# The last eight rows of a prefix-sum kernel's input loaded by SyncE's queue instead of GpSimd's

## The chip, the cores and the metric

The kernel runs on one core of one Trainium2 chip. The metric is the device time of one execution in microseconds (us). Before the change it is 668.23 us, the median of 3 runs (667.75 to 668.69). A profile of one execution comes with a trace of it.

## The reference

```python
def setup_inputs():
    B, H, W = 4, 4224, 4224
    return {"x": np.random.randn(B, H, W).astype(np.float32)}

def reference(x):
    B, H, W = x.shape
    ps = np.cumsum(np.cumsum(x, axis=1), axis=2)
    N = min(H, W)
    diag = np.diagonal(ps, axis1=1, axis2=2)
    return np.cumsum(diag, axis=1).astype(np.float32)
```

For each of four 4224x4224 matrices the two-dimensional prefix sum is taken, its diagonal is read, and the diagonal is summed up once more. Output i of a batch is therefore a sum over the diagonal entries up to i, and each of those is a sum over a square corner of the matrix. All of x (285 MB in fp32) has to be read once; the output is 4x4224 numbers.

## The kernel before

**Main part.** P is 128 and N is 4224. Rows are taken in groups of 384 (GW), of which there are 11 (NG). A strip is 768 rows, 6 on each partition, cast from fp32 to bf16 by the load itself: `load_rows` (L75) issues it on GpSimd's (POOL's) queue. The pool `strips` has three buffers (NBUF), so a load is issued when the strip three places earlier has been used up. For each strip, `add_up` lets TensorE sum columns right of the diagonal into the tile `d`, lets VectorE (DVE) mask the block on the diagonal (L353, L354), and lets ScalarE (ACT, `act_sum`, L262) and DVE (`row_sums`, L267) sum the rows left of it. After each batch a short chain over `d` gives the carries between groups and the batch's sums (L477, L479).

**The last batch** (b = 3) has four whole strips, called s = 0 to 3 here. A fifth strip buffer takes two half strips of 384 rows (h = 0 and 1). A sixth, which is the buffer of s = 2 again, takes the rest of the rows in small pieces, all on POOL's queue:

- `part_a`, two blocks of 128 rows in strip rows 0 and 1, in two loads of 2160 and 1536 columns (L433), for all but the last 528 columns, which SyncE (SP) loaded as fp32 at the very start (`head`, L68);
- `part_b`, the last 128 rows, 4096 columns (TB) of them, in strip row 2. They are four blocks of 32 rows (R). A row is cut into four pieces of 1024 columns, so that a block of 32 rows covers 128 partitions. The blocks 0, 1 and 2 are one load each. Block 3 is two loads of 768 and 256 columns (bcut), all at L444.

Strip row 3 is scratch (`spare`); rows 4 and 5 are unused.

The order of the instructions on each engine is the order in which the program writes them. On DVE the second half strip (h = 1) follows right on the `row_sums` of the first (h = 0). At the very end block 3 is summed by `act_sum` and two `pair_sum` (L276) into the three columns of `esum`; three small products with `weights4` add these to `fin_e`, the last 32 outputs; DVE copies them (L562), and SP sends them out (L563). SP's queue holds in this order: `head`, the sums of the first three batches (L540), those of the last (L543), and the three last pieces of the output (L546, L557, L563).

Of the kernel before, what the change touches and what calls it, by code (L numbers as in the profile page):

```python
# [8 lines left out]
FP32 = mybir.dt.float32  # L9
# [8 lines left out]
def kernel(  # L18
# [14 lines left out]
    nc = tc.nc  # L33

    B, H, W = x.shape
    N = H
    P = 128
# [7 lines left out]
    TB = N - P  # L45
# [7 lines left out]
    last = ctx.enter_context(tc.tile_pool(name="last", bufs=1))  # L53
# [16 lines left out]
    def strip_tile():  # L70
        return strips.tile([P, F2, N], BF16, name="strip")

    def load_rows(o, b, r0):
        f = o.shape[1]
        nc.gpsimd.dma_start(  # L75
            out=o, in_=x[b, r0 : r0 + f * P, :].rearrange("(p f) w -> p f w", f=f)
        )
# [20 lines left out]
    def upper_mask(f):  # L98
# [22 lines left out]
        out=um1,  # L121
        in_=um1,
# [10 lines left out]
        out=ident,  # L133
        in_=ident,
# [13 lines left out]
    def counted(name, rows, width, pieces):  # L148

        ti = consts.tile([P, GW], I32, name="counted")[:rows, :width]  # L150
        for c0, c1, base, step, cm in pieces:
            nc.gpsimd.iota(
                ti[:, c0:c1],
                pattern=[[step, c1 - c0]],
                base=base,
                channel_multiplier=cm,
            )
        tf = consts.tile([rows, width], FP32, name=name)
        nc.gpsimd.tensor_copy(out=tf, in_=ti)
        return tf  # L160
# [6 lines left out]
    def between_groups(name, turned):  # L167
# [25 lines left out]
    weights = counted("weights", P, GW, [(0, GW, 1, 1, -1)])  # L193
    nc.gpsimd.affine_select(
        out=weights,
        in_=weights,
# [8 lines left out]
    R = P // 4  # L205
# [3 lines left out]
        out=steps, in_=steps, scalar=2, op=ALU.arith_shift_right  # L209
    )  # L210
    weights4 = consts.tile([P, P], FP32, name="weights4")
# [5 lines left out]
    def matmul(o, lhsT, rhs, start=False):  # L217
        nc.tensor.matmul(  # L218
            o, lhsT=lhsT, rhs=rhs, start=start, stop=False, skip_group_check=True
        )  # L220
# [36 lines left out]
    def act_sum(acc, src, own=None):  # L257
        w = src.shape[-1]
        dump = own
        if dump is None:  # L260
            dump = src
        nc.scalar.activation(  # L262
            out=dump[:, :w], in_=src, func=ACT.Copy, accum_out=acc
        )

    def row_sums(acc, src):
        nc.vector.reduce_sum(out=acc, in_=src, axis=AX.X)  # L267

    pairs = []

    def pair_sum(acc, src):

        w = src.shape[-1] // 2
        pair = last.tile([P, w], FP32, name=f"pair{len(pairs)}")
        pairs.append(pair)
        nc.vector.scalar_tensor_tensor(  # L276
            out=pair[:, :w],
            in0=src[:, :w],
            scalar=1.0,
            in1=src[:, w:],  # L280
            op0=ALU.mult,
            op1=ALU.add,
            accum_out=acc,
        )
# [17 lines left out]
        nc.vector.memset(rows3[i], 0.0)  # L302


    asum = last.tile([P, 2, 2], FP32, name="asum")
    dtot = last.tile([P, 1], FP32, name="dtot")
    hu = last.tile([P, 3], FP32, name="hu")
    hmu = last.tile([P, 3, GW], BF16, name="hmu")
    for h in range(2):
        w = GW - h * P  # L310
# [6 lines left out]
    for b in range(B):  # L317
# [10 lines left out]
        def row_of(j):  # L328
            return (j + t0) % NG
# [12 lines left out]
        def add_up(strip, f, r0, acc, um, fs=0, wp=0, ws=0, by_rows=False):  # L342


            nw = f * P // GW
            g = r0 // GW
            hi = r0 + f * P
            for j in range(g + nw + by_rows, NG):
                for q in range(f):
                    columns(j, 0, GW, strip[:, q, j * GW : (j + 1) * GW], q > 0)  # L350
            mu = mup.tile([P, f, f * P], BF16, name=f"mu{f}")
            block = strip[:, :, r0:hi]
            nc.vector.tensor_mul(out=mu, in0=block, in1=um)  # L353
            nc.vector.tensor_sub(out=block, in0=block, in1=mu)  # L354
            if by_rows:
                rowed = mup.tile([P, GW], FP32, name="rowed")
                row_sums(
                    rowed,
                    strip[:, :, hi : hi + GW].rearrange("p q c -> p c q"),
                )  # L360
            for h in range(nw):
                for q in range(f):
                    columns(g + h, 0, GW, mu[:, q, h * GW : (h + 1) * GW], q > 0)
            if by_rows:
                k = row_of(g + nw)
                matmul(d, sel_f[:, NG - 1 - k : 2 * NG - 1 - k], rowed)
            if fs:
                for q in range(fs):
                    act_sum(acc[:, q : q + 1], strip[:, q, :hi])
                row_sums(acc[:, fs:], strip[:, fs:, :hi])  # L370
            else:
                for q in range(f):
                    act_sum(acc[:, q, 0:1], strip[:, q, wp:ws])
                row_sums(acc[:, :, 1], strip[:, :, ws:hi])
# [4 lines left out]
        for s in range(ns):  # L379
            strip = prefetched.pop(0) if prefetched else None  # L380
            if strip is None:
                strip = strip_tile()
# [14 lines left out]
        for h in range(2):  # L397
            ps = slice(h * HP, (h + 1) * HP)
            k = row_of(h)
            nc.vector.tensor_copy(  # L400
                out=r6[ps, k : k + 2 * ns : 2, :], in_=a6[ps]
            )

        strip = strip_tile()
        if whole:
            load_rows(strip[:, :F], b, T0)
            add_up(strip[:, :F], F, T0, r3[:, LG], um3, F - 1)
        else:


            for h in range(2):
                load_rows(strip[:, h * F : h * F + F], b, T0 - (2 - h) * GW)
            add_up(strip[:, :F], F, T0 - 2 * GW, r3[:, row_of(LG - 2)], um3, F - 1)
            ready = psum_s.tile([P, 512], FP32, name="fold")
            for i in range(28):
                matmul(ready, ident_h, um6[:, i % F2, :512], start=True)
            fold_g = psum_s.tile([P, F, 160], FP32, name="fold")
            wp, ws = 1920, 1920 + 1248
            fold_in(fold_g, strip[:, F:], 0, wp, 160, start=True)
            parts = last.tile([P, F, 3], FP32, name="parts")  # L420
            add_up(strip[:, F:], F, T0 - GW, parts, um3, wp=wp, ws=ws)
            row_sums(parts[:, :, 2], fold_g)
            row_sums(r3[:, row_of(LG - 1), :], parts)

        if not whole:

            strip = strip_tile()
            part_a = strip[:, 0:2]
            part_b = strip[:, 2, :TB].rearrange("p (s c) -> p s c", s=4)
            spare = strip[:, 3, :]  # L430
            acuts = [(1536, N - HC), (0, 1536)]
            for c0, c1 in acuts:
                nc.gpsimd.dma_start(out=part_a[:, :, c0:c1], in_=src_a[:, :, c0:c1])  # L433
            CB = TB // 4
            bcut = 768
            for sb, c0, c1 in (
                (0, 0, CB),
                (1, 0, CB),
                (2, 0, CB),
                (3, 0, bcut),  # L440
                (3, bcut, CB),
            ):
                r0 = TB + sb * R
                nc.gpsimd.dma_start(  # L444
                    out=part_b[:, sb, c0:c1],
                    in_=x[b, r0 : r0 + R, :TB].rearrange("r (k c) -> r k c", k=4)[
                        :, :, c0:c1
                    ],
                )

            fold_a = psum_s.tile([P, 2, 256], FP32, name="fold_a")
            c0, c1 = acuts[0]
            fcuts = [c0, c0 + 768, c0 + 2048, c1]
# [13 lines left out]
        c1 = mup.tile([NG, GW], FP32, name="c1")  # L467
# [10 lines left out]
        for i, (to, src) in enumerate(((c1, d), (c2, c1))):  # L478
            nc.vector.tensor_tensor_scan(  # L479
                out=to,  # L480
# [14 lines left out]
        fin_e = psum_s.tile([1, R], FP32, name="fin_e")  # L495
# [7 lines left out]
        def weigh_b(rows, w, r0=0, start=False):  # L503

            m = P - R - r0
            matmul(fin_b[:, r0:], rows, w[..., :m], start=start)
            matmul(fin_e, rows, w[..., m : m + R], start=start)


        c0, c1 = acuts[1]  # L510
# [5 lines left out]
        nc.scalar.copy(out=by, in_=by_ps)  # L516
        weigh_b(dtot, weights, start=True)
        weigh_b(ones_col[0:1], last_sums[0:1, M0:])


        row_sums(asum[:, :, 1], fold_a)
# [10 lines left out]
        esum = last.tile([P, 3], FP32, name="esum")  # L532
        act_sum(bsum[:, 0, 0:1], part_b[:, 1, :512], spare[:, :512])
        pair_sum(bsum[:, 0, 1:2], part_b[:, 1, 512:])
        for i in (1, 0):
# [5 lines left out]
            out=out[:LB, :].rearrange("b (g i) -> g b i", i=GW), in_=whole_sums  # L541
        )
        nc.sync.dma_start(  # L543
            out=out[b, :T0].rearrange("(g i) -> g i", i=GW), in_=last_sums[1:NG]
        )
        nc.sync.dma_start(  # L546
            out=out[b, T0 : T0 + M0].unsqueeze(0), in_=yl[:, :M0]
        )
        for i in (1, 0):
            weigh_b(bsum[:, 1, i : i + 1], weights4, 2 * R)  # L550


        act_sum(esum[:, 0:1], part_b[:, 3, :320], spare[:, 960:1280])
        pair_sum(esum[:, 1:2], part_b[:, 3, 320:bcut])
        pair_sum(esum[:, 2:3], part_b[:, 3, bcut:])
        nc.scalar.copy(out=yl[:, M0:E0], in_=fin_b)
        nc.sync.dma_start(  # L557
            out=out[b, T0 + M0 : T0 + E0].unsqueeze(0), in_=yl[:, M0:E0]
        )
        for k in (1, 0, 2):  # L560
            matmul(fin_e, esum[:, k : k + 1], weights4[:, :R])
        nc.vector.tensor_copy(out=ye, in_=fin_e)  # L562
        nc.sync.dma_start(out=out[b, T0 + E0 : N].unsqueeze(0), in_=ye)  # L563

# [29 lines left out]
```

## Time and profile before

| | us |
|---|---|
| median of 3 runs | 668.23 |
| the profiled execution | 667.48 |
| its span, first to last instruction | 665.4 |
| DVE busy | 334.5 (50%) |
| PE busy | 211.2 (32%) |
| ACT busy | 154.5 (23%) |
| POOL busy | 31.7 (5%) |
| traffic of POOL's load queue (q0) | 99.9% of 16 DMA engines' span |

The table is read from the bottom: no compute engine is busy for more than half of the time, while the 16 DMA engines work nearly all of it. The mean rate is 215 GB/s as written, and the HBM is read at 429 GB/s, twice as much, because the loads cast four-byte numbers to two-byte ones. The trace also holds a record of every DMA packet with its queue, size, start and duration, but not the number of the DMA engine that carried it.

### The profile page before, as it was taken

Reading aid. Unit: us, or ns where it says so; the run is one execution under the profiler, and the core shown is the slowest. Engines: PE = TensorE matmul, PEld = TensorE weight load, DVE = VectorE, ACT = ScalarE, POOL = GpSimd, SP = SyncE. Lnnn points to the kernel's source line nnn. Section 1 sums busy time; section 2 is a strip of 40 time slices with the busy share of each in tenths; the row PEclk is TensorE's granted clock in tenths of the full one; section 3 lists DMA queues with packets and bytes.
Section 4 is the critical chain, followed back from the end, with each engine's and each line's share of the span. In section 5 each row is a group of like instructions: output and inputs, shape, how many; then the busy total and the mean of one; then the engine's idle time right before and its main releaser. Section 6 shows DMA issues by size and latency. Waiting matters only on the chain.

```text
span 665.4 us, 2519 instructions
## 1 busy us (share of the span) xinstructions
PE 211.2 (32%) x997; PEld 97.2 (15%) x998; DVE 334.5 (50%) x160; ACT 154.5 (23%) x145; POOL 31.7 (5%) x60
## 2 busy tenths in 40 slices
PE   0071422303107143230311623404022253250458
PEld 0030210101103021010110311201001121120224
DVE  4141727466914163655782325456487323251746
ACT  0010203133511020322450102123154010221443
POOL 4200000000000000000000000000000000001000
PEclk9995857655558585665555957567565595765789
DMA  9999999999999999999999999999999999999998
GB/s 203 219 219 219 219 219 218 213 213 210 220 219 218 219 219 219 218 215 213 212 220 218 219 216 219 219 218 217 212 216 216 218 218 219 218 218 216 216 205 164
DMA packets 7666, 143.24 MB, mean 215 GB/s; under 512 B 698, under 2 KB 998, under 8 KB 2150
## 3 DMA queue, kind: packets, MB, share of 16 engines
q0 software_dynamic: 7312, 142.47, 99.9%
q1 hardware_dynamic: 342, 0.61, 0.3%
q8 instruction: 8, 0.13, 0.1%
q14 instruction: 4, 0.03, 0.0%
HBM read 285.47 MB, written 0.07 MB: 429 GB/s over the span
## 4 chain that ended last, share of the span: by engine, by line
DVE 42%; another core or an unknown queue 40%; DMA 11%; ACT 3%; issue 1%; PE 1%; POOL 1%; DVEq 0%; ACTq 0%; POOLq 0%
DVE acc L267 19%; DMA strip<-in_x_dram 11%; DVE mu L353 7%; DVE strip L354 7%; DVE rowed L267 7%; ACT strip L262 3%; PE d L218 0%; DVE c L479 0%; DVE whole_sums L479 0%; POOL strip L444 0%; DVE pu L267 0%; DVE whole_sums L287 0%; POOL strip L433 0%; DVE rows L400 0%
## 5 line engine op out<-in xcount | busy, mean ns | idle before, releaser
L262 ACT ACTIVATE strip<-strip 128x768 bf16<-128x768 bf16 (+9 forms) x71 | 150.3, 2118 | 481.7 <-DVE strip L354 450.8
L353 DVE TENSOR_TENSOR mu<-strip,um 128x4608 bf16<-128x4608 bf16 (+1 forms) x24 | 52.4, 2183 | 294.3 <-DMA strip<-in_x_dram 294.2
L225 PEld LDWEIGHTS <-sel 128*11 128x11 bf16 x643 | 66.5, 103 | 475.0 <-issue 445.1
L267 DVE TENSOR_REDUCE acc<-strip 128x3 f32<-128x2304 bf16 (+4 forms) x19 | 134.8, 7094 | 0.2
L218 PE MATMUL d<-strip,sel 128*11 128x384 bf16 x90 | 37.2, 413 | 286.9 <-DMA strip<-in_x_dram 286.9
L225 PE MATMUL d<-strip,sel 128*11 128x384 bf16 x441 | 115.6, 405 | 13.8 <-DMA strip<-in_x_dram 13.8
L354 DVE TENSOR_TENSOR strip<-strip,mu 128x4608 bf16<-128x4608 bf16 (+1 forms) x24 | 52.4, 2183 | 1.5
L267 DVE TENSOR_REDUCE rowed<-strip 128x384 f32<-128x2304 bf16 x12 | 49.3, 4110 | 0.0
L218 PE MATMUL d<-mu,sel 128*11 128x384 bf16 x43 | 15.9, 370 | 103.1 <-DVE mu L353 103.1
L225 PE MATMUL d<-mu,sel 128*11 128x384 bf16 x200 | 45.9, 364 | 0.0
L75 POOL DMA_DIRECT2D strip<-in_x_dram x23 | 15.7, 684 | 534.7 <-DVE acc L267 287.9
L218 PE MATMUL d<-rowed,sel_f 128*11 128x384 f32 x24 | 11.5, 568 | 21.9 <-DVE rowed L267 21.9
L267 DVE TENSOR_REDUCE rows<-strip 128x1 f32<-128x4224 bf16 (+1 forms) x4 | 17.4, 4353 | 0.1
L218 PEld LDWEIGHTS <-sel 128*11 128x11 bf16 x134 | 13.5, 101 | 22.7 <-issue 10.2
L262 ACT ACTIVATION_READ_ACCUMULATOR strip<-strip 128x1 f32 x71 | 13.2, 186 | 0.0
L218 PE MATMUL d<-ident,rows 128*11 128x128 f32 x24 | 5.7, 374 | 16.5 <-ACT strip L262 16.5
L267 DVE TENSOR_REDUCE pu<-d 11x1 f32<-11x384 f32 x4 | 2.2, 545 | 14.1 <-PE d L218 14.1
L218 PE MATMUL fold<-um,ident_h 128*128 128x512 bf16 x27 | 6.3, 392 | 0.3 <-issue 0.3
L262 ACT ACT_TABLE_LOAD x1 | 1.3, 1283 | 19.7 <-DMA strip<-in_x_dram 19.7
L102 POOL TENSOR_SCALAR_AFFINE_SELECT um<-um 128x4608 bf16<-128x4608 bf16 (+1 forms) x2 | 5.2, 2612 | 7.3 <-DVE um L101 7.3
L101 DVE MEMSET um<- 128x4608 bf16 (+1 forms) x2 | 4.9, 2458 | 1.1 <-issue 1.1
L218 PEld LDWEIGHTS d<-rowed,sel_f 128*11 128x11 f32 x24 | 1.5, 91 | 26.8 <-DVE rowed L267 26.4
(114 smaller groups left out, 75.8 us busy)
## 6 DMA issues: line engine op xcount, KB each, us to landing
strip<-in_x_dram POOLq DMA_DIRECT2D x18, 6336.0 KB, 73.5
strip<-in_x_dram POOLq DMA_DIRECT2D x7, 3168.0 KB, 57.5
strip<-in_x_dram POOLq DMA_DIRECT2D x1, 1080.0 KB, 51.6
strip<-in_x_dram POOLq DMA_DIRECT2D x1, 768.0 KB, 54.6
strip<-in_x_dram POOLq DMA_DIRECT2D x3, 256.0 KB, 55.9
head<-in_x_dram SPq DMA_DIRECT2D x1, 528.0 KB, 3.9
strip<-in_x_dram POOLq DMA_DIRECT2D x1, 192.0 KB, 43.2
strip<-in_x_dram POOLq DMA_DIRECT2D x1, 64.0 KB, 28.6
```

The source lines that it names most:

```text
L75: nc.gpsimd.dma_start(out=o, in_=x[b, r0 : r0 + f * P, :].rearrange("(p f) w -> p f w", f=f))
L101: nc.vector.memset(um, 1.0)
L102: nc.gpsimd.affine_select(out=um, in_=um, compare_op=ALU.is_gt, fill=0.0, base=0, pattern=[[-1, f], [1, f * P]], channel_multiplier=-f,)
L218: nc.tensor.matmul(o, lhsT=lhsT, rhs=rhs, start=start, stop=False, skip_group_check=True)
L225: te.add_instruction(mybir.InstMatmult(start_tensor_calc=False, stop_tensor_calc=False, tile_position=(0, 0), tile_size=(P, P if lhsT.shap ...
L262: nc.scalar.activation(out=dump[:, :w], in_=src, func=ACT.Copy, accum_out=acc)
L267: nc.vector.reduce_sum(out=acc, in_=src, axis=AX.X)
L353: nc.vector.tensor_mul(out=mu, in0=block, in1=um)
L354: nc.vector.tensor_sub(out=block, in0=block, in1=mu)
```

## The change

Of the last 32 rows of the last batch only 24 stay in block 3 on POOL's queue. The loads of that block cover 96 partitions instead of 128, and so do the sums over it. The other 8 rows (E) come by SP's queue, uncast, each row whole: 4096 fp32 numbers on one of the partitions 0 to 7, in strip rows 4 and 5 of the same sixth buffer. That buffer is now taken from the pool ahead of the first half strip's `add_up`, not behind the second's. One DVE reduction sums the 8 rows (`end_sums`), and one small product adds them to the last 8 columns of `fin_e`.

SP's load waits for what the buffer waits for, the last use of s = 2. It stands second in SP's queue, ahead of the output of the first three batches. On DVE the new reduction stands between the reduction of h = 0 and the mask of h = 1. On TensorE the new product stands ahead of the `by` products. The other engines keep their order.

```diff
-        pair = last.tile([P, w], FP32, name=f"pair{len(pairs)}")
+        pair = last.tile([P, w], FP32, name=f"pair{len(pairs)}")[: src.shape[0]]
...
+    E = 8
+    end_sums = last.tile([E, 1], FP32, name="end_sums")
...
+            tail = strip_tile()
+            ends = tail[:E, 4:6, :].rearrange("p q c -> p (q c)").bitcast(FP32)
+            nc.sync.dma_start(out=ends[:, :TB], in_=x[b, N - E : N, :TB])
             add_up(strip[:, :F], F, T0 - 2 * GW, r3[:, row_of(LG - 2)], um3, F - 1)
+            row_sums(end_sums, ends[:, :TB])
...
-            strip = strip_tile()
+            strip = tail
...
-            for sb, c0, c1 in (
-                (0, 0, CB),
-                (1, 0, CB),
-                (2, 0, CB),
-                (3, 0, bcut),
-                (3, bcut, CB),
+            for sb, rows, c0, c1 in (
+                (0, R, 0, CB),
+                (1, R, 0, CB),
+                (2, R, 0, CB),
+                (3, R - E, 0, bcut),
+                (3, R - E, bcut, CB),
             ):
                 r0 = TB + sb * R
                 nc.gpsimd.dma_start(
-                    out=part_b[:, sb, c0:c1],
-                    in_=x[b, r0 : r0 + R, :TB].rearrange("r (k c) -> r k c", k=4)[
-                        :, :, c0:c1
-                    ],
+                    out=part_b[: 4 * rows, sb, c0:c1],
+                    in_=x[b, r0 : r0 + rows, :TB].rearrange(
+                        "r (k c) -> r k c", k=4
+                    )[:, :, c0:c1],
                 )
...
+        matmul(fin_e[:, R - E :], end_sums, weights[:E, :E])
...
-        act_sum(esum[:, 0:1], part_b[:, 3, :320], spare[:, 960:1280])
-        pair_sum(esum[:, 1:2], part_b[:, 3, 320:bcut])
-        pair_sum(esum[:, 2:3], part_b[:, 3, bcut:])
+        PE = 4 * (R - E)
+        act_sum(esum[:PE, 0:1], part_b[:PE, 3, :320], spare[:PE, 960:1280])
+        pair_sum(esum[:PE, 1:2], part_b[:PE, 3, 320:bcut])
+        pair_sum(esum[:PE, 2:3], part_b[:PE, 3, bcut:])
...
         for k in (1, 0, 2):
-            matmul(fin_e, esum[:, k : k + 1], weights4[:, :R])
+            matmul(fin_e, esum[:PE, k : k + 1], weights4[:PE, :R])
```

## The prediction

> **What bounds the kernel now.** I read the page from the back: the DMA queues first, because the DMA row of the slices is full, then the chain, then the last microseconds in the timeline.
>
> ```profile
> DMA  9999999999999999999999999999999999999998
> q0 software_dynamic: 7312, 142.47, 99.9%
> q1 hardware_dynamic: 342, 0.61, 0.3%
> q8 instruction: 8, 0.13, 0.1%
> ```
>
> POOL's queue (q0) fills all 16 DMA engines for the whole span. SP's queue (q1) and the instruction fetches (q8) share the same engines. So the bound is the work of the DMA engines, and bytes moved from q0 to q1 are not gone. The chain of waits says the same: DVE pieces in it are followed by long waits for strips, and it ends so (start, us, what):
>
> ```profile
> 605.43 13.44 another core or an unknown queue
> 618.86 0.28 issue
> 619.15 43.18 DMA strip<-in_x_dram
> 662.33 0.02 issue
> 662.35 0.41 DVE pair L276 x2
> 662.76 0.04 issue
> 662.81 0.48 PE fin_e L218 x6
> 663.29 0.02 issue
> 663.31 0.18 DVE ye L562
> ```
>
> Block 3's first load ends the wait at 662.33; then come two pair sums, three products, a copy and the output. The timeline of DVE shows that the second pair follows the first at once:
>
> ```profile
> 662.35 0.39 DVE L276 SCALAR_TENSOR_TENSOR pair<-strip 128x224 f32<-128x224 bf16 x1
> 662.67 0.08 DVE L276 DVE_READ_ACCUMULATOR pair<-strip 128x1 f32 x1
> 662.70 0.29 DVE L276 SCALAR_TENSOR_TENSOR pair<-strip 128x128 f32<-128x128 bf16 x1
> ```
>
> Then the single packets. A 25,344-byte packet of q0 (50,688 bytes read) takes 1.886 us, and each engine runs them back to back. Each q0 load ends with 16 completion packets, one per engine. For the load of h = 1 these spread over 1.46 us: nine engines lie 0 to 0.71 us behind the first, seven lie 1.16 to 1.46 behind. The cause shows in the records: the last two 16,384-byte fetches of q8 inside the strips (0.945 and 0.935 us each) moved one engine each from 0.29 to 1.41 and from 0.18 to 1.29, that is by 1.11. Seven fetches, seven late engines. A load is complete when its last engine is, so **the latest engine sets the end**, and it matters whom the change loads.
>
> The 33 packets of SP's first output ran on 11 engines, three each (11 completions), and shifted 11 engines by about 0.2 us; the five unshifted ones include three late ones, the latest (1.46) among them. So four late engines (1.22, 1.28, 1.41, 1.43) are among the 11. The 10-row output left 10 completions. I take it that 8 rows go to 8 engines, one 16,384-byte row each, the first 8 of those 11. Only three of the 11 remain outside, so at least one late engine gets a row.
>
> **Part by part.**
>
> *Removed from q0.* Block 3 goes from 128 pieces to 96, from 8 descriptors per engine to 6 in each of its two loads. A 1536-byte packet takes 134.5 ns, a 512-byte one 59.5, so each engine saves 2 x 134.5 + 2 x 59.5 = 0.39 us. That all 16 engines still share is assumed.
>
> *Given back at once.* Shorter loads end 0.39 earlier, but the first pair sum takes 0.39 itself and cannot start earlier than the first load of block 3, which gains 0.27 (2 x 134.5). The second pair sum therefore starts at best at 662.35 - 0.27 + 0.37 = 662.45 instead of 662.70. (0.35 us lie between the two starts today.) So the removal is worth 0.25, and I use 0.23, since ACT's sums (0.47 and 0.58 us, back to back there) allow no more. ACT and DVE take as long for 96 partitions as for 128.
>
> *Added to q1.* One 16,384-byte row on each of eight engines. At q0's read rate a row costs 16,384 / 50,688 x 1.886 = 0.61 us, the lower bound for an engine that carries one. The nearest row is the instruction fetch of the same size: 0.94 us, and 1.11 by the shift that it left. I take 1.11. The upper bound: all eight go to eight neighbouring partitions, and if they get in each other's way there so far that one lands after the other, the last engine is held for 8 x 0.61 = 4.9 us; two at a time it is 2.4. I stay with 1.11, the row of the same size on the same engines. A cost below zero is excluded: the packets of the first output shifted their engines by their own length (3 x 65 ns, 0.2 us).
>
> [...]
>
> *When it runs.* SP waits for the last use of s = 2, as POOL does for `part_a`, issued at 602.35. The load of `head` took 3.9 us to landing on idle queues; a busy engine adds the packet it is in, up to 1.9. So it lands at about 606 to 611, while its data are first wanted at 640. Behind it in SP's queue the first output moves from 520 to about 602: nobody waits for it, and its packets cost the same.
>
> *DVE.* The sum of 1056 fp32 took 1.25 us and that of 3456 bf16 took 3.75, so 4096 take 4.4 to 4.9. It starts when h = 0 is summed:
>
> ```profile
> 636.04 3.75 DVE L267 TENSOR_REDUCE rows<-strip 128x1 f32<-128x3456 bf16 x1
> 648.93 0.76 DVE L353 TENSOR_TENSOR mu<-strip,um 128x1152 bf16<-128x1152 bf16 x1 [9.13 <-DMA strip<-in_x_dram]
> ```
>
> The 9.13 us of waiting for h = 1 cover it with 4 us over. Without that cover it would cost its 4.4 to 4.9, and the mask of h = 1 with all behind it would be late. *TensorE* gets one more small product, as `fin_e` beside it, 0.22 us. It stands behind work that was waiting for loads anyway, and TensorE reaches the last products 0.35 us ahead of DVE's pair. I cost it at nothing; at worst 0.22.
>
> *Sum.* I take the latest of the four to have a row. It comes to 1.43 + 1.11 = 2.54 behind the first, where the latest now is at 1.46: +1.08. Less 0.23 for the smaller loads: **+0.85 us**. (With the least late of the four it is +0.64.) Span 665.4 to 666.25, profiled execution 667.48 to 668.33; the median is 0.75 above the profiled execution, so 668.23 to 669.1.
>
> **The rivals.**
>
> 1. *The row is cheap.* At 0.61 us with the least late engine (1.22 + 0.61 = 1.83) the sum is +0.37 - 0.23 = +0.14, 668.4; if the row is hidden whole, it is -0.23, 668.0. For it: 0.61 is the rate that nearly all packets have. Against: the two packets of this size on these engines cost 1.11.
>
> 2. *Slower: the rows crowd each other* on the way into eight neighbouring partitions, and an engine that is held there holds its q0 packets too. At two at a time a row costs 2.4 us, 1.43 + 2.4 - 1.46 - 0.23 = +2.1, 670.4; one after the other up to 672.9. For it: every other load of this kernel spreads its engines over 128 partitions, and nothing shows that eight engines may write so few at full speed. Against: the engines are out of step by up to 1.5 us, so the rows do not all meet. From about 1.6 us per row on (1.43 + 1.6 - 1.46 - 0.23 = 1.34) it is a loss of more than 0.2%.
>
> 3. *The smaller loads are no smaller for an engine.* 24 rows are no multiple of 16. If they run on 12 engines, 8 descriptors each as before, an engine that takes part in both saves nothing: +1.08, 669.3. For it: 11 rows ran on 11 engines and 10 on 10, so the outer count decides on q1. Against: every q0 load here shows 16 completions, but all have outer counts divisible by 16. [...]
>
> 4. *A gain*: the change is meant to shorten the tail, and if the late engines were spared a row, all would end 0.39 earlier, worth 0.23. Even lateness spread over all engines alike would give no more than some 0.7 (1.46 less the mean of 0.72). No row shows a gain over 1.3 us; the chance for it is for what I do not see.
>
> **How the numbers follow.** 0.2%, 1.34 us, is about what a measurement of this kernel can tell from no change. Chances: the forecast 0.29, rival 1 0.16, rival 2 0.34, rival 3 0.13, a gain 0.08. Slower: all of rival 2; of rival 3 0.07, since there a row of 1.4 us is enough; of the forecast 0.02 for its upper end; 0.43 in all. Faster: 0.06 of the gain. The same: the rest, 0.27 + 0.16 + 0.06 + 0.02 = 0.51. The forecast is 669.1. The range goes from 667.9, rival 1 at its best, to 671.0, rival 2 with a row at 3 us; about one tenth lies outside at either end.
>
> **What the profile after would show.** Right: a q1 load of 128 KB from SP issued at about 602 and landed before 612; eight records of 16,384 bytes of 0.6 to 1.1 us on q1; the `end_sums` reduction near 640, 4.4 to 4.9 us, and still a wait for h = 1 behind it; the completions of the h = 1 load spread over about 2.5 us instead of 1.46; the last pair sum at about 663.5. Wrong: records of 2 us and more (rival 2), a spread that stays near 1.5 (rival 1, or late engines spared), four engines that complete a load of block 3 without a data packet of it (rival 3). The whole would be wrong if the DVE sum ended behind h = 1's landing, or the end were no longer set by block 3.

## The result and the profile after

The changed kernel takes 669.49 us, the median of 15 runs (669.14 to 670.17); the kernel before, run beside it, 668.10 (15 runs). The ratio is 1.0022, 95% interval 1.0014 to 1.0030: 1.39 us slower (by the interval, 0.9 to 2.0 us). The profiled execution took 669.28 with a span of 667.2 (before 667.48 and 665.4).

The page's DMA lines, after:

```profile
DMA  9999999999999999999999999999999999999997
q0 software_dynamic: 7312, 142.40, 99.7%
q1 hardware_dynamic: 358, 0.74, 0.4%
q8 instruction: 8, 0.13, 0.1%
```

The work has only changed queues: q1 has 128 KB more (0.74 MB against 0.61), and the engines are as full as before (q0 takes 99.7% against 99.9%). SP issues the rows when the buffer is free, and the first three batches' output right behind (the timeline of SP: start, us):

```profile
601.86 0.34 SPq L417 DMA_DIRECT2D strip<-in_x_dram  x1
602.24 0.33 SPq L547 DMA_DIRECT2D out_dram<-whole_sums  x1
```

On DVE the rows' sum takes 4.40 us, and DVE still waits 4.74 us behind it. But h = 1, which started DVE at 648.93 before, now starts it at 650.30:

```profile
641.17 4.40 DVE L267 TENSOR_REDUCE end_sums<-strip 8x1 f32<-8x4096 f32 x1
650.30 0.76 DVE L355 TENSOR_TENSOR mu<-strip,um 128x1152 bf16<-128x1152 bf16 x1 [4.74 <-DMA strip<-in_x_dram]
...
663.75 0.41 DVE L546 TENSOR_TENSOR yl<-fin_a,last_sums 1x256 f32<-1x256 f32 x1
664.09 0.37 DVE L276 SCALAR_TENSOR_TENSOR pair<-strip 96x224 f32<-96x224 bf16 x1
664.40 0.07 DVE L276 DVE_READ_ACCUMULATOR pair<-strip 96x1 f32 x1
664.40 0.29 DVE L276 SCALAR_TENSOR_TENSOR pair<-strip 96x128 f32<-96x128 bf16 x1
```

So in this profile **1.37 us are lost by the time h = 1 lands**; the medians differ by 1.39. The chain of waits no longer ends in a load, but in the work that h = 1 starts (start, us, what):

```profile
650.26 0.58 PE fold L218
650.84 4.40 PE fold L225 x11
...
662.07 0.59 DVE asum L267
...
662.90 0.81 PE fin_a L218 x4
...
664.67 0.31 PE fin_e L218 x8
665.01 0.18 DVE ye L570
```

It is a near tie, however, and block 3's loads still count. Its last load, by the DMA lines (KB, us to landing) and POOL's timeline, before and then after:

```profile
strip<-in_x_dram POOLq DMA_DIRECT2D x1, 64.0 KB, 28.6
634.10 0.53 POOL L444 DMA_DIRECT2D strip<-in_x_dram  x1 [14.42 <-DMA strip<-in_x_dram]
...
strip<-in_x_dram POOLq DMA_DIRECT2D x1, 48.0 KB, 28.8
635.55 0.57 POOL L450 DMA_DIRECT2D strip<-in_x_dram  x1 [14.36 <-DMA strip<-in_x_dram]
```

The trace's semaphore records put these two landings at 662.68 and 664.38. The second pair sum starts 0.02 us behind each, at 662.70 and 664.40, and DVE's last copy, `ye`, goes from 663.31 to 665.01. All three move by 1.70 us: 1.37 by h = 1 and 0.33 in the loads behind it.

The packet records say how the delay at h = 1 came about. The eight rows took 0.62, 0.77, 0.86, 1.09, 1.19, 1.30, 1.34 and 1.51 us, 8.68 in all, and 2.56 us from the first start to the last end. In the same stretch **17 packets of q0 took 1.93 to 2.68 us instead of 1.886**, 6.80 us too much in all. At 608.0 us fifteen of these run at once, and only eight engines have a row (the load left eight completions), so engines without a row were held too. The DMA engines thus spent 15.5 us of engine time on 128 KB.

The records also show 64 four-byte packets more on q0 than before (592 against 528).

### The profile page after: what moved, and what is told of

It reads as the page before. It is cut to its first block, busy times and chain, and to the rows that moved or that the text cites. A ratio compares the mean times of both kernels' runs of the same rounds, so it can differ in the third digit from the quotient of the medians.

```text
span 667.2 us, 2530 instructions
## 1 busy us (share of the span) xinstructions
PE 212.1 (32%) x999; PEld 97.6 (15%) x1000; DVE 338.7 (51%) x161; ACT 154.5 (23%) x145; POOL 31.8 (5%) x60
## 3 DMA queue, kind: packets, MB, share of 16 engines
q0 software_dynamic: 7312, 142.40, 99.7%
## 4 chain that ended last, share of the span: by engine, by line
another core or an unknown queue 43%; DVE 38%; PE 10%; DMA 5%; ACT 3%; issue 1%; POOL 0%; DVEq 0%; ACTq 0%; POOLq 0%
DVE acc L267 16%; DVE rowed L267 7%; DVE mu L355 6%; DVE strip L356 6%; PE d L225 5%; DMA strip<-in_x_dram 5%; ACT strip L262 3%; PE d L218 2%; PE fold L218 1%; PE fold L225 1%; DVE c L485 0%; DVE whole_sums L485 0%; DVE pu L267 0%; DVE whole_sums L287 0%
## 5 line engine op out<-in xcount | busy, mean ns | idle before, releaser
L262 ACT ACTIVATION_READ_ACCUMULATOR strip<-strip 128x1 f32 (+1 forms) x71 | 13.2, 186 | 0.0
```

Of the source, the lines that this page charges most:

```text
L262: nc.scalar.activation(out=dump[:, :w], in_=src, func=ACT.Copy, accum_out=acc)
```

## The experiments

Each kernel was timed in 5 rounds beside the kernel before. Kernels that load no rows by SP show how far one profile can be trusted: in the four of them h = 1 started DVE between 648.75 and 649.18 (in the kernel before at 648.93). Where rows crowd, profiles differ more: the same eight rows gave 650.30 in the change and 649.98 in the next kernel.

**The load alone.** The change with the sum and the product taken out and block 3 left whole:

```diff
-            row_sums(end_sums, ends[:, :TB])
-        matmul(fin_e[:, R - E :], end_sums, weights[:E, :E])
-                (3, R - E, 0, bcut),
-                (3, R - E, bcut, CB),
+                (3, R, 0, bcut),
+                (3, R, bcut, CB),
-        PE = 4 * (R - E)
+        PE = 4 * R
```

Expected: 

> The kernel before with SP's load of 8 rows added and nothing taken away: block 3 keeps its 32 rows, the 8 rows that land by SP are not summed (they are read twice, and only block 3's copy counts). My theory: the rows held all engines, and the smaller block 3 saved the late engines nothing, so the load alone costs all of the change: h = 1 lands 1.3 to 1.4 us later, ratio about 1.002. Rival (the smaller block 3 was worth 0.23 us, and its gain hid part of the rows' cost): 1.7 us, ratio 1.0025. Rival (the DVE sum or the product cost something): the ratio is well below 1.002.

Measured: 1.0023 (1.0014 to 1.0031), as the change. Rows of 0.62 to 1.39 us, 19 stretched packets, h = 1 at 649.98, 1.05 later. The load is the whole loss; the DVE sum, the product and the smaller block 3 add up to nothing that can be seen.

**The smaller block 3 alone.** SP's load, its sum and its product are out, block 3 keeps its 24 rows:

```diff
-            nc.sync.dma_start(out=ends[:, :TB], in_=x[b, N - E : N, :TB])
-            row_sums(end_sums, ends[:, :TB])
-        matmul(fin_e[:, R - E :], end_sums, weights[:E, :E])
```

Expected: 

> Block 3 with 24 rows, and the last 8 rows loaded by nobody (the last 8 outputs lack them). My theory (24 rows run on 12 engines with 8 data packets each, as before): the end moves by less than 0.1 us, ratio 1.000, though 128 KB less is read; four engines per load carry no data packet. Rival (16 engines, 6 packets each): 0.23 to 0.39 us less, ratio 0.9995, and each engine's last stretch is a quarter shorter in the packet records.

Measured: 1.0001 (0.9992 to 1.0010). Reading 128 KB less gains nothing. The time alone can't tell 0 from 0.2 us; the records can. From the last completion of h = 1 to that of block 3 the four kernels with 32 rows take 13.91 to 14.43 us, the five with 24 rows 13.84 to 14.20, and the five with 16 rows 13.28 to 13.30. So 24 rows land about as late as 32. Here too are 64 four-byte packets more than before, and none more in any kernel whose block 3 has 32 or 16 rows. They fit 12 engines with 8 data packets and one completion each, and four that carry eight fillers of four bytes instead: 2 loads x 4 engines x 8 = 64. That is my reading of the count, since no record names its engine; in the change the first eight fillers begin within 0.04 us, at 660.26 to 660.30.

**The same rows on partitions that lie apart.** The load alone, as above, but on every fourth partition:

```diff
-            ends = tail[:E, 4:6, :].rearrange("p q c -> p (q c)").bitcast(FP32)
+            ends = tail[0 : 4 * E : 4, 4:6, :].rearrange("p q c -> p (q c)").bitcast(FP32)
```

Expected: 

> As e1_load_only (block 3 whole, the 8 rows read twice and not summed), the same 8 whole rows on the same 8 engines, but on partitions 0, 4, 8 to 28 instead of 0 to 7. Crowding theory: each row takes about 0.6 us, no packet of the other queue is stretched, h = 1 lands 0.4 to 0.7 us later than before, ratio 1.001 or less. Rival (a whole row of 16,384 bytes is slow by itself, or 8 engines with a row each are the cost): rows of 0.6 to 1.4 us and stretched packets as in e1_load_only, ratio 1.002.

Measured: 1.0007 (0.9998 to 1.0016), 0.42 us. All eight rows took 0.624 us, and not one packet of q0 was stretched. The timeline of DVE:

```profile
649.53 0.76 DVE L355 TENSOR_TENSOR mu<-strip,um 128x1152 bf16<-128x1152 bf16 x1 [9.05 <-DMA strip<-in_x_dram]
```

h = 1 comes 0.60 later than before, the price of one uncrowded row. Queue, engine count, packet size and place are those of the load alone; only the partitions differ. **That shows the crowding**: of its 1.05 us in the profile, 0.45 go with the partitions, and 1.04 of the 1.46 by the medians. What it is about the partitions 0 to 7 that makes the rows crowd, no run here tells.

**Sixteen rows.** `E = 16` in the change, on partitions 0 to 15, and block 3 has 16 rows. Every engine has a row if each row again has an engine of its own, as the 8, 10 and 11 rows of this queue's other transfers left 8, 10 and 11 completions.

```diff
-    E = 8
+    E = 16
```

Expected: 

> The change with 16 rows by SP instead of 8, so that all 16 engines get a row, on partitions 0 to 15; block 3 has 16 rows, 4 data packets per engine and load, which saves every engine 0.78 us by the packet records. Crowding theory: rows of 0.6 to 1.5 us and twice as many stretched packets, about 1.9 us per engine added and 0.78 saved, +0.8 to +1.2 us, ratio 1.0015. Rival (the 8 engines and the 12-engine loads were the whole cost): 0.61 added and 0.78 saved, ratio 0.9998. The DVE sum is as long as in the change (4096 numbers), on 16 partitions.

Measured: 1.0032 (1.0019 to 1.0044), more than expected. The rows took 0.62 to 1.81 us, and 20 packets of q0 were stretched, up to 3.06, by 12.4 us in all. It lost 2.2 us, although by that reading every engine has the same number of rows, and block 3 is half as large. The even share did not cure the crowding.

**The rows in pieces over all partitions.** First 8 rows on 8 engines, 16 pieces of 1024 bytes each; then the same with the pieces outermost, so that 16 engines have half a row each (by the same reading of the completions):

```diff
-            ends = tail[:E, 4:6, :].rearrange("p q c -> p (q c)").bitcast(FP32)
-            nc.sync.dma_start(out=ends[:, :TB], in_=x[b, N - E : N, :TB])
+            ends = tail[:, 4, :512].bitcast(FP32)
+            nc.sync.dma_start(
+                out=ends,
+                in_=x[b, N - E : N, :TB].rearrange("r (k c) -> r k c", k=16),
+            )
...
-                in_=x[b, N - E : N, :TB].rearrange("r (k c) -> r k c", k=16),
+                in_=x[b, N - E : N, :TB].rearrange("r (k c) -> k r c", k=16),
```

(Each has a matrix of weights for its order of the pieces.)

Expected: 

> As the change, but each of the 8 rows goes in 16 pieces of 1024 bytes to 16 partitions, so that the load covers all 128 partitions while one row still belongs to one of 8 engines. Crowding theory (eight neighbouring partitions take the rows too slowly and hold every engine): the rows cost about 0.6 to 0.8 us on eight engines, no packet of the other queue is stretched, h = 1 lands 0.4 to 0.7 us later, ratio 1.0005 to 1.001. Rival (eight engines with a row each are the cost, wherever it lands): h = 1 lands 1.1 us later or more, ratio 1.002. The DVE sum is 256 numbers instead of 4096, which neither theory counts.

> As e3_spread_8, but with the pieces in the other order, so that all 16 engines carry 8 pieces of 1024 bytes, half a row each. Crowding theory and the theory of few engines alike: 0.3 to 0.4 us per engine, evenly, h = 1 lands 0.3 to 0.4 later, ratio 1.0005. A ratio of 1.002 here would say that the cost is neither the eight partitions nor the eight engines, but the load at that place or the 24-row block.

Measured: 1.0015 (1.0006 to 1.0023) and 1.0010 (1.0001 to 1.0019). No packet was stretched in either, so the crowding theory holds there; its price does not. I had expected 0.6 to 0.8 us for the first, and it cost 0.96. A piece of 1024 bytes takes 59 ns, 16 of them 0.94 us, where the whole row takes 0.624. (In its profile h = 1 came 1.56 later, but there one engine lay 1.90 behind before any row.) On 16 engines 8 x 59 ns = 0.47; h = 1 came 0.51 later.

**Sixteen rows in pieces of 2048 bytes over all partitions**, 8 pieces on each of 16 engines (against the first of the two above):

```diff
-    E = 8
+    E = 16
-            ends = tail[:, 4, :512].bitcast(FP32)
+            ends = tail[:, 4, :1024].bitcast(FP32)
-                in_=x[b, N - E : N, :TB].rearrange("r (k c) -> r k c", k=16),
+                in_=x[b, N - E : N, :TB].rearrange("r (k c) -> r k c", k=8),
```

Expected: 

> As e5_rows_16, but each row goes in 8 pieces of 2048 bytes to 8 partitions, so that 16 engines write all 128 partitions: even, uncrowded, and block 3 truly smaller. Crowding theory: 8 packets of about 0.09 us per engine (0.7 us) added, 0.78 saved: within 0.3 us of the kernel before, ratio 1.000. It is the version that should be as good as the kernel before or a little better. If it is as slow as the change, neither crowding nor the number of engines is the cause.

Measured: 1.0014 (1.0006 to 1.0023): a miss. 8 pieces at 96 ns are 0.77 us per engine, and h = 1 came 0.98 later; the 0.78 that block 3 saves behind it did not come back. Why not, the next two ask.

**Block 3 cut to 16 rows, nothing in their place** (against the change; the last 16 outputs lack these rows):

```diff
-    E = 8
+    E = 16
-            nc.sync.dma_start(out=ends[:, :TB], in_=x[b, N - E : N, :TB])
-            row_sums(end_sums, ends[:, :TB])
-        matmul(fin_e[:, R - E :], end_sums, weights[:E, :E])
```

Expected: 

> The kernel before with block 3 cut to 16 rows (4 data packets per engine and load) and the last 16 rows loaded by nobody (the last 16 outputs lack them). Theory 1: the chain of products and sums that starts when h = 1 lands sets the end nearly as much as the loads behind it, so that 0.78 us less of loads on every engine move the end by 0.3 us at most, ratio 0.9995 to 1.000, and the pair sums of block 3 wait for no load. Rival: the loads alone set the end, 0.6 to 0.8 us less, ratio 0.999.

Measured: 0.9998 (0.9989 to 1.0007). Every engine has an estimated 0.78 us less to load at the very end (four packets of 134.5 ns and four of 59.5), and the median falls by 0.22, less than the noise. The timeline of DVE of this kernel shows why:

```profile
661.71 0.46 DVE L276 SCALAR_TENSOR_TENSOR pair<-strip 128x288 f32<-128x288 bf16 x1 [0.79 <-DMA strip<-in_x_dram]
662.09 0.08 DVE L276 DVE_READ_ACCUMULATOR pair<-strip 128x1 f32 x1
662.09 0.41 DVE L542 TENSOR_TENSOR yl<-fin_a,last_sums 1x256 f32<-1x256 f32 x1
662.43 0.37 DVE L276 SCALAR_TENSOR_TENSOR pair<-strip 64x224 f32<-64x224 bf16 x1
662.74 0.07 DVE L276 DVE_READ_ACCUMULATOR pair<-strip 64x1 f32 x1
662.74 0.28 DVE L276 SCALAR_TENSOR_TENSOR pair<-strip 64x128 f32<-64x128 bf16 x1
```

The last wait for a load is block 2's (0.79 us). From there DVE runs without a gap: block 2's pair, `yl`, and block 3's two pairs, whose data lie there already. In the kernel before, the same lines read:

```profile
661.45 0.46 DVE L276 SCALAR_TENSOR_TENSOR pair<-strip 128x288 f32<-128x288 bf16 x1 [0.80 <-DMA strip<-in_x_dram]
661.83 0.08 DVE L276 DVE_READ_ACCUMULATOR pair<-strip 128x1 f32 x1
661.83 0.41 DVE L539 TENSOR_TENSOR yl<-fin_a,last_sums 1x256 f32<-1x256 f32 x1
```

Block 3's pair started at 662.35, 0.52 us behind the start of `yl`; with 16 rows it starts 0.34 behind it. So block 3's loads held that pair back by 0.18 us, and a smaller block 3 can gain some 0.2 us there, no more, whatever it saves in loads. The profiles show about that: from the start of h = 1 to that of `ye` 14.38 us before and 14.15 here. My theory named the chain that h = 1 starts; what the lines show is a shorter one, from block 2's load on.

**Sixteen rows early.** The pieces of 2048 bytes into a tile of their own, behind SP's first load; the later load of them is gone:

```diff
+    ends = last.tile([P, 512], FP32, name="ends")
+    nc.sync.dma_start(
+        out=ends, in_=x[LB, N - 16 : N, :TB].rearrange("r (k c) -> r k c", k=8)
+    )
```

Expected: 

> As e6_spread_rows_16 (16 rows uncast by SP over all 128 partitions, block 3 of 16 rows), but into a tile of its own, issued right behind the first load of SP at the very start. Theory: the packets cost their engines the same 0.6 to 0.7 us there, except for what they find idle before POOL's first packet at 4 us; h = 1 lands 0 to 0.7 us later than before; ratio 0.9995 to 1.001. Rival (the place right ahead of h = 1 is what hurts in e6_spread_rows_16): as the kernel before or 0.5 us faster, ratio 0.999 to 1.000.

Measured: 1.0009 (1.0000 to 1.0018), h = 1 at 649.44, 0.51 late. The same pieces near the end made it 0.98 late; the medians lose 0.60 us here and 0.96 there. So at the start of the kernel the packets are not free either. Whether they cost less there is open, since the two intervals overlap.

**More unused products on TensorE.** In the change's profile the 11 products of h = 1 took 4.6 us against 3.5 before, after a longer wait (5.68 us against 5.34). So the 28 unused products that precede them were made 40, in the change, in the kernel before, and in the one with block 3 cut to 16 rows:

```diff
-            for i in range(28):
+            for i in range(40):
```

Expected: 

> The change, with 40 instead of 28 unused products on TensorE ahead of h = 1, so that it idles some 3 us instead of 5.7 before the products of h = 1. In the profiles so far those products took 3.5 us after a wait of up to 5.34 us and 4.6 after one of 5.68 or more. Theory: part of the change's loss is that TensorE, waiting longer for h = 1, comes out slower, 1.1 us in a chain that had some 0.6 to spare; then the 11 products take 3.6 us or less here and the ratio falls from 1.0022 to about 1.0016. Rival (the late rows alone): still 1.002.

> The kernel before with 40 instead of 28 unused products. Theory: its wait is 5.34 us in the profile shown, near the edge; some of its executions lie beyond it. Then 0 to 0.4 us less, ratio 0.9995 to 1.000. Rival (it makes no difference, the loads set the end): 1.000.

> e8_block3_16 (16 of block 3's rows left out, the last 16 outputs lack them) with 40 instead of 28 unused products. If a slow TensorE were what kept the smaller block 3 from showing, this would be 0.5 us faster than the kernel before, ratio 0.999. By my theory the chain behind h = 1 and the loads ahead of block 3 set the end all the same: 0.9995 to 1.000.

Measured: 1.0025 (1.0014 to 1.0037), 1.0000 (0.9991 to 1.0009) and 0.9994 (0.9985 to 1.0003). The wait fell to 1.96, 2.43 and 2.14 us, and the change was no faster. The ratio can't tell the 1.0016 of the theory from 1.0022, but the trace can: the second pair of block 3 starts here at 665.01, 0.03 us behind its load's landing, as it did 0.02 behind it in the change. So the load is what it waits for, and the theory of the slower TensorE falls. The products took 4.0 us there, 3.8 in the kernel before; the length of the wait is not all that sets them. (In this profile of the change h = 1 starts at 651.19, 2.26 later than before. But the strip that landed ahead of the rows was complete 0.82 later than before already, at 589.49, which leaves 1.44.)

No version was found that clearly beats the kernel before. The last one is nearest, but it leaves out 16 rows.

## Why the prediction was right, and where its steps were not

- *Right*: the engines were the bound (q0 still takes 99.7%), bytes moved to another queue stayed work, and the latest engine decided. 669.1 was forecast with a range up to 671.0; 669.49 was measured. Slower by over 0.2% had a chance of 0.43, and the result lies on that line. The hit says little for the sum: the range held rivals 1 to 3 as well (668.4, 670.4, 669.3), and rival 3's number is the nearest.
- *The row, priced at 1.11 us*: the rows took 0.62 to 1.51, 1.09 in the mean. That the price fits is luck (in the load alone the mean is 0.86), and its reason was wrong. An uncrowded row takes 0.624, so the lower bound of 0.61 was close. The instruction fetch of the same size (0.94 us) is not the like of it.
- *The missing term*: nothing in the sum held engines without a row, or the other queue's packets on engines with one. They lost 6.80 us of engine time, nearly as much as the rows took. So the latest engine came to +1.37 where the sum had +1.08. That was rival 2's mechanism, though at less than two thirds of its price: with 2.4 us for a late engine it comes to +2.37 at h = 1. The rows began over 1.05 us, so they did not all meet. No run shows the two rows at a time on which the 2.4 us rest: 8.68 us of rows within 2.56 us are 3.4 at a time in the mean, and none of the eight took over 1.51. From the first start to the last end the load alone took 3.11, and the rows four apart, held by nothing, 1.99, so that stretch is no measure of the crowding. With the partitions four apart the hold was gone.
- *The removal, -0.23*: this step failed, and it was nothing that can be seen. If the 24 rows run on 12 engines (rival 3, which the 64 fillers fit), an engine that takes part in both loads saves nothing; block 3 landed about as late behind h = 1 as with 32 rows (13.84 to 14.20 us against 13.91 to 14.43). The size was about right for a block that does land earlier: with 16 rows the profiles gain 0.23 and 0.21 us between h = 1 and `ye`, and `yl` (L539) leaves no more. But the second pair of before was misread. It did not merely follow the first; it began 0.02 us behind the landing of its own load.
- *Sum by the runs*: +1.37 at h = 1 and 0 for block 3, against +1.39 by the medians. The sum of +0.85 was too small by 0.29 for the rows and 0.23 for the removal.
- *Costed at nothing, and so it was*: the DVE sum (4.40, forecast 4.4 to 4.9, with 4.74 us of waiting left), block 3's sums over 96 partitions (0.47 us on ACT, 0.37 and 0.29 on DVE, against 0.47, 0.39 and 0.29 over 128), the product, the output that moved from 520 to 602.
- *The marks*: the rows issued at 601.9, the last of them done at 608.0 and the load's completions by 610.4 (forecast 606 to 611); the completions of h = 1 spread over 2.2 us (forecast 2.5); the last pair sum at 664.40 (forecast 663.5). The sign for rival 3, engines that complete a load of block 3 without data, was there by that reading of the fillers. The end "no longer set by block 3" would have made the whole wrong: the chain of waits says so, but the landings say that block 3 sets it still.
- *Open*: between h = 1's landing and the end the profiled execution loses 0.33 us more than before, in the loads behind h = 1: their last landing moved as much as the end did. An instruction fetch of 0.32 us fell in that stretch, at 660.0, and may be the reason. The medians show no such loss, so it may belong to that execution alone.

## What to carry to other kernels

Here the DMA engines were full (q0 took 99.7%), and a load moved to an idle queue was not moved off the path (1.39 us lost). Ask which engines carry such a load, which of them are late already (by up to 1.46 us here), and which partitions they write: beside eight rows on partitions 0 to 7, 17 packets of the other queue took up to 2.68 us instead of 1.886; beside the same rows four partitions apart none did. Before a load at the end is made shorter, read what the engine that uses it is doing in the microsecond before: here an unrelated 0.41 us addition left some 0.2 to gain. Look twice at a row count that 16 does not divide: with 24 rows block 3 landed 13.84 to 14.20 us behind h = 1, with 32 rows 13.91 to 14.43, with 16 rows 13.28 to 13.30.

## What the runs showed of the hardware that was not expected

- Eight uncast rows of 16,384 bytes on partitions 0 to 7 lengthened 17 packets of the other queue from 1.886 us to as much as 2.68; sixteen rows on partitions 0 to 15 lengthened 20, up to 3.06; eight rows on partitions 0, 4 to 28 lengthened none.
- Block 3's two loads of 24 rows, in four pieces per row, sent 64 four-byte packets beyond the 16 completions of each; with 16 and 32 rows they sent none.
- Uncast pieces of 1024 bytes took 59 ns and of 2048 bytes 96 ns, beside 39 and 78 for the same bytes within a whole row (624 ns for 16,384).
